# Making all adaLN vectors on TensorE and leaving GpSimd only its memsets, in a two-block transformer kernel

## The chip, the cores and the metric

The kernel runs on one core of one Trainium2 chip. The metric is the time of one execution on the device in microseconds (us), as the median of several runs. The core has five engines that matter here: TensorE (PE in the profile, its weight loads PEld), VectorE (DVE), ScalarE (ACT), GpSimd (POOL) and SyncE (SP), which issues all DMAs of this kernel. Each engine works through its own queue in order, and engines wait for each other by semaphores.

## The reference

Two transformer blocks of two layers each are applied to 256 tokens of 1024 features, in float32.

In a layer of the first block a conditioning vector `c` gives the adaLN vector `mod = silu(c) @ ada_w[l] + ada_b[l]`, 6144 numbers, which are split into six parts of 1024: a shift, a scale and a gate for the attention half, and the same for the MLP half. The attention half computes

```
h = rms_norm(x, norm1_g) * (1 + sc1) + sh1
da_q, da_k, da_v, dn_q, dn_k, dn_v, dn_z, dn_b, dn_a, gates = split(h @ w_in)
y_a = diff_attention(da_q, da_k, da_v, ...)
y_b = gated_deltanet(dn_q, dn_k, dn_v, dn_z, dn_b, dn_a, ...)
x = x + gt1 * ((g_a * (y_a @ w_branch_a) + g_b * (y_b @ w_branch_b)) @ w_out)
```

and the MLP half `x = x + gt2 * (relu(h @ w_mlp1)**2 @ w_mlp2)` with an `h` made of `sc2` and `sh2`. The delta rule works on chunks of 64 tokens: the inverse of a triangular matrix for each chunk, and then a scan over the four chunks, in both directions.

A layer of the second block has three kinds of attention over one projection, an output projection, and a mixture of 16 experts in which each expert picks 32 tokens; its weights are 12 MB an expert. The output is normed at the end.

## The kernel before

**Order of issue.** Nothing is issued as it is written. A class `Plan` records all operations of a stretch of the program, and a list schedule (`Plan.schedule`) then gives each engine, among the operations whose operands are there, the one with the longest way to the end by fixed costs and latencies. The first block is one such stretch. Every tile has a kind (`a8` 2048 columns, `s4` 1024, `w2` 512, `w1` 256, `t` 64, and the PSUM banks `acc` and `pg`), and the schedule also hands out the slots. In the first block there are five `a8` slots for loads of weights, eight `s4` slots for split weights, three `acc` banks for dense products and five `pg` banks for all else, and fourteen `w1` slots (8 and `W1X` = 6). Slots of `a8`, `s4` and `acc` are given out in program order.

**Weights.** A `Stream` holds the loads in the order of their use, 1 MB each. A weight that goes into a dense product is split in two fp32r halves: `act(hi, r)` on ScalarE and `tt(lo, r, hi, subtract)`, on VectorE or, by the table `LO`, on GpSimd:

```
LO = dict(dn=(V, G), gate=(V, V, G))
LO["in"] = (G, G, V)
```

`dense` then does three fp32r matmuls of 128x128 by 256 columns for each chunk of 128 rows.

**adaLN.** 48 units of 256 columns by 1024 rows. The first eight (the parts that the first norm needs) are loaded into `w2` tiles and done on TensorE: eight matmuls with `c32`, which is silu(c) repeated in 32 columns, fill four groups of 32 rows of a bank, and a product with `quad` adds up the groups. The other forty are items of the `Stream`: twelve of layer 0 between the loads of the attention stage, four of layer 0 and all 24 of layer 1 between the loads of layer 0's MLP. By `ADA` they go in turn to VectorE (a multiplication and seven multiply-adds of 128x256) and to GpSimd (one product of 128x2048 and three sums); four units' results are summed over the partitions by TensorE.

**A layer of the first block.** `Norm.finish` makes `h`; `dnp` makes the delta rule's q, k, v with a convolution (`conv`, VectorE); then `deltanet`'s steps are woven with `fill`, which holds the products for the differential attention, that attention itself (`diffattn`), the gates and `w_branch_a`. After that come `w_branch_b`, `w_out` with the residual add (`resid`), and the MLP in four quarters (`up`, `down`). In `deltanet`, GpSimd has the masks' products (`row`, `kkm`, `pd`, `cm`), `kb`, `kd`, the decay of the state and sums of the output; in `diffattn` the low halves of q and k; in the second block the low halves of the attention's outputs, `halves` (the normed tokens, split, for the gather) and small copies.

**The second block** has no `acc` banks; its `a8` slots take loads of expert weights that run ahead, and the tiles `xn`, `xh`, `xl` of `halves`.

In the profile nearly all instructions have line 596, where the schedule issues them; they are told apart by the names of tiles. There `block` is a tile of kinds `a8` and `s4`, `quarter` one of `w2`, `w` one of `w1`, `t` a small one, `ps` a PSUM bank, `x` the residual, `cT` silu(c), `mod` the adaLN vectors.

Of the kernel before, what the change touches and what calls it, by code (L numbers as in the profile page):

```python
# [10 lines left out]
F32R = mybir.dt.float32r  # L11
# [18 lines left out]
W1X, NT = 6, 10  # L30


# ---------------------------------------------------------------- host layout
def _units(w, n=2):
    """[K, N] -> [N/(128 n), 128 (k in chunk), n, K/128, 128]: lhsT units of n column chunks."""
    k, c = w.shape
    a = w.reshape(k // 128, 128, c // (128 * n), n, 128).transpose(2, 1, 3, 0, 4)
    return np.ascontiguousarray(a).reshape(c // (128 * n), 128, -1)


def _rows(w, kc):
    """[K, N] -> [K/(128 kc), 128, kc, N]: rhs units of kc row chunks."""
# [5 lines left out]
def _cols(v):  # L48
    """[n*128] -> [128, n]"""
    return np.ascontiguousarray(v.reshape(-1, 128).T)  # L50
# [13 lines left out]
def _shape_consts():  # L64
    """constants of the program, packed by the time that they are needed: c0 always, c1 and c2 per block"""
# [71 lines left out]
def _bias(rpb):  # L137
    """[4, 15, 31] -> [4, 128 (q in tile), 2 * 256]: bias of q over k, NEG outside q's window"""
# [10 lines left out]
def _layout(i):  # L149
# [25 lines left out]
    a["ada"] = st(lambda l: _rows_n(i["ada_w"][l], 256))  # L175
# [55 lines left out]
def _rows_n(w, n):  # L231
    """[1024, N] -> [N/n, 128, 8, n]"""
    k, c = w.shape
    a = w.reshape(8, 128, c // n, n).transpose(2, 1, 0, 3)
    return np.ascontiguousarray(a).reshape(c // n, 128, 8 * n)
# [35 lines left out]

class Tile:
# [7 lines left out]
class Plan:  # L280
    """Operations are recorded in program order and issued in the order of a list schedule: each engine takes,
    among the operations whose operands are there, the one with the longest way to the end. Costs and latencies
    are the guide's, in ns; they depend on shapes alone. A tile's slot is given out ahead of program order only if
    program order could still go on from there. Products that fill half of the array or less are not issued in long
    rows while others are ready: the array's clock falls when it is used little."""
# [17 lines left out]
    # -------------------------------------------------------- recording  # L303
# [22 lines left out]
    def box(r):  # L326
        """(what, partitions from, to, columns from, to)"""
# [37 lines left out]
    def add(self, eng, name, fn, args, kw):  # L365
# [4 lines left out]
        if eng == "P" and self.cols(ins[0]) < 128 and name == "matmul":  # L370
            p = self.ops[-1]
            rng = outs[0].ap.ap[0][1], outs[0].ap.offset // outs[0].ap.ap[0][0]
            if p.group and p.outs[0].t is outs[0].t and rng not in p.group:
                p.group.append(rng)
                self.access(p, n - 1, ins, outs)
                p.calls.append((fn, args, kw))
# [10 lines left out]
        o.eng, o.calls, o.dma, o.deps, o.succ, o.start, o.tiles = eng, [(fn, args, kw)], None, set(), [], None, []  # L387
# [38 lines left out]
    # -------------------------------------------------------- scheduling  # L426
# [3 lines left out]
    def keys(self, n0):  # L430
        """time to the end by a list schedule that runs backwards, in which every engine is single"""
# [33 lines left out]
    def schedule(self, slots):  # L465
        """slots: per kind of tile, the time at which each slot gets free"""
# [24 lines left out]
        def fit(e, t, dur):  # L491
            """the first time from t on at which engine e is idle for dur"""
# [8 lines left out]
        def can(i, t):  # L501
            """the earliest time from t on at which operation i's tiles have slots"""
# [76 lines left out]
    def flush(self, place, slots, issue):  # L579
        """schedules what has been recorded, into what waits and has gaps; place(kind, slot): the slot's memory"""  # L580
# [4 lines left out]
        for e in "PVAG":  # L585
            self.eng_at[e] = max(f for s, f in self.busy[e])
            self.busy[e] = []
        self.waiting.sort(key=lambda z: (self.ops[z[0]].start, z[0]))
        for i, place in self.waiting:
# [5 lines left out]
            for fn, args, kw in o.calls:  # L595
                self.tc.keep_in_program_order(fn(*map(real, args), **{k: real(v) for k, v in kw.items()}))  # L596
# [1545 lines left out]
```

## Time and profile before

| | |
|---|---|
| median of 3 runs | 2407.26 us (2403.64 to 2407.43) |
| profiled execution | span 2408.3 us, 38449 instructions |
| TensorE, weight loads | 82%, 60% of the span busy |
| VectorE | 48% |
| ScalarE | 33% |
| GpSimd | 19%, 278 instructions |
| mean granted TensorE clock | 0.862 of full speed |
| read from HBM | 617 MB |

The profiled execution is one execution of its own; its time is its span. Busy shares are means over stages that differ much, so they are read by stage below. A matmul's end is modelled, so a busy TensorE isn't TensorE at its peak.

### The profile page before, as it was taken

What the parts mean: (1) busy time and instruction counts of PE and PEld (TensorE: products, weight loads), DVE (VectorE), ACT (ScalarE), POOL (GpSimd) and SP (SyncE); (2) the same over time, 40 slices, a digit from 0 to 9 for tenths busy, and PEclk for the clock granted to TensorE, in tenths of its full rate; (3) what the DMA queues carried; (4) which work ended last, traced back from release to release, by engine and by line L of the source; (5) the groups of instructions that cost most, each with busy time, mean ns of one, the idle gap of its engine ahead of it and who ended that gap; (6) DMA issues with size and microseconds to landing.
All of it is one profiled execution on the core that took longest, in us unless ns stands there. A gap on an engine that the chain in (4) does not pass through costs nothing. (4 is left out here: it accounts for less than half of the span.)

```text
span 2408.3 us, 38449 instructions
## 1 busy us (share of the span) xinstructions
PE 1984.8 (82%) x16200; PEld 1437.7 (60%) x16200; DVE 1159.4 (48%) x1908; ACT 786.9 (33%) x1508; POOL 465.6 (19%) x278
## 2 busy tenths in 40 slices
PE   8688987778989999999999887666769988666665
PEld 5677777777987777999986542222237644222222
DVE  5998478999789623775557410000006731000001
ACT  4363343433457323654456210000015521000001
POOL 1555354455133312000020210000002111000000
PEclk7897898788999768999999888887779988877777
DMA  8354224566633310645544699999995579999997
GB/s 315 124 188 128 105 106 158 210 229 254 237 121 132 116 36 18 247 158 178 203 153 167 274 420 420 421 421 420 421 420 212 209 281 420 420 421 420 420 421 313
DMA packets 108253, 622.36 MB, mean 258 GB/s; under 512 B 27184, under 2 KB 28464, under 8 KB 34992
## 3 DMA queue, kind: packets, MB, share of 16 engines
q1 hardware_dynamic: 108080, 619.90, 65.4%
q8 instruction: 127, 2.08, 0.3%
q14 instruction: 46, 0.38, 0.0%
HBM read 617.24 MB, written 2.62 MB: 257 GB/s over the span
## 5 line engine op out<-in xcount | busy, mean ns | idle before, releaser
L596 PE MATMUL ps<-quarter,block 128*128 128x256 f32 (+1 forms) x5760 | 868.4, 304 | 72.5 <-DVE quarter L596 23.6
L596 PEld LDWEIGHTS ps<-quarter,block 128*128 128x128 f32 x5760 | 786.2, 205 | 114.9 <-issue 28.2
L596 PE MATMUL ps<-block,block 128*32 128x256 f32 (+4 forms) x5204 | 546.5, 431 | 137.9 <-DMA block<-in_w_up_dram 95.1
L596 PEld LDWEIGHTS ps<-block,block 128*32 128x32 f32 (+2 forms) x5204 | 274.4, 136 | 354.7 <-DMA block<-in_w_up_dram 159.3
L596 DVE TENSOR_TENSOR block<-block,block 128x1024 fp32r<-128x1024 f32 (+2 forms) x262 | 364.7, 1398 | 130.6 <-PE ps L596 73.1
L596 ACT ACTIVATE block<-block 128x1024 fp32r<-128x1024 f32 (+2 forms) x312 | 319.1, 1028 | 321.9 <-PE ps L596 292.8
L596 ACT ACTIVATE w<-ps 128x256 f32<-128x256 f32 (+1 forms) x138 | 52.3, 382 | 819.0 <-PE ps L596 818.9
L596 DVE TENSOR_TENSOR w<-w,ps 128x256 f32<-128x256 f32 x64 | 26.9, 421 | 544.3 <-ACT w L596 537.8
L596 POOL TENSOR_TENSOR block<-block,block 128x1024 fp32r<-128x1024 f32 x46 | 117.0, 2551 | 794.3 <-ACT block L596 387.8
L596 PE MATMUL ps<-block,w 128*32 128x256 f32 x2048 | 176.0, 500 | 25.8 <-ACT w L596 13.3
L596 PE MATMUL ps<-quarter,quarter 64*64 64x64 f32 (+6 forms) x1312 | 166.8, 304 | 6.9 <-DVE quarter L596 6.9
L596 PEld LDWEIGHTS ps<-block,w 128*32 128x32 f32 x2048 | 76.9, 142 | 116.2 <-issue 49.8
L596 PEld LDWEIGHTS ps<-quarter,quarter 64*64 64x64 f32 (+3 forms) x1312 | 113.2, 177 | 53.2 <-issue 20.0
L596 ACT ACTIVATE quarter<-quarter 128x512 f32<-128x512 f32 (+2 forms) x188 | 116.2, 628 | 85.0 <-DVE quarter L596 82.5
L596 ACT ACTIVATE quarter<-ps 128x512 f32<-128x512 f32 (+1 forms) x136 | 79.5, 592 | 151.2 <-PE ps L596 133.8
L596 DVE SCALAR_TENSOR_TENSOR w<-block,cT,w 128x256 f32<-128x256 f32 x140 | 126.5, 903 | 2.2
L596 DVE TENSOR_SCALAR w<-c,slot 128x256 f32<-128x256 f32 x32 | 12.5, 411 | 234.9 <-PE ps L596 234.8
L596 PE MATMUL ps<-w,w 32*128 32x256 f32 x512 | 106.7, 418 | 15.4 <-ACT w L596 15.1
L596 POOL TENSOR_TENSOR block<-block,cT 128x2048 f32<-128x2048 f32 x20 | 76.5, 3825 | 136.8 <-DVE w L596 41.0
L596 PEld LDWEIGHTS ps<-w,w 32*128 32x128 f32 x512 | 55.5, 185 | 69.2 <-issue 35.4
L596 DVE TENSOR_TENSOR quarter<-quarter,ps 128x512 f32<-128x512 f32 (+1 forms) x80 | 49.0, 629 | 84.7 <-PE ps L596 80.0
L596 POOL TENSOR_TENSOR block<-block 128x1024 f32<-128x1024 f32 (+1 forms) x40 | 85.2, 2131 | 2.4
(169 smaller groups left out, 1604.8 us busy)
## 6 DMA issues: line engine op xcount, KB each, us to landing
block<-in_w_gate_dram SPq DMA_DIRECT2D x144, 1024.0 KB, 19.8
block<-in_w_up_dram SPq DMA_DIRECT2D x128, 1024.0 KB, 19.8
block<-in_w_down_dram SPq DMA_DIRECT2D x128, 1024.0 KB, 19.8
block<-in_w_m_dram SPq DMA_DIRECT2D x64, 1024.0 KB, 4.8
block<-in_ada_dram SPq DMA_DIRECT2D x40, 1024.0 KB, 6.1
block<-in_w_dn_dram SPq DMA_DIRECT2D x16, 1024.0 KB, 4.8
block<-in_w_o_dram SPq DMA_DIRECT2D x16, 1024.0 KB, 7.0
block<-in_w_in_dram SPq DMA_DIRECT2D x12, 1024.0 KB, 12.1
```

The lines of the kernel that those rows point to most:

```text
L596: self.tc.keep_in_program_order(fn(*map(real, args), **{k: real(v) for k, v in kw.items()}))
```

## The change

All of adaLN goes to TensorE. The weights are laid out anew: a unit is now 256 rows by 1024 columns, so that four units make one of the six parts of 1024 columns. Each unit's eight matmuls add to one PSUM bank, which is held from the first of four units to the last; then one copy and two products with a four-column `quad` bring the rows into place, and one addition adds the bias. In the first block's `Stream` each layer now carries its own units 8 to 23, and layer 0's MLP the first eight of layer 1; in the MLP one comes after every second load and not after every load. All elementwise work of GpSimd goes to VectorE, memsets stay. `halves` does the scaling and the subtraction in one instruction, without the tile `xn`. `W1X` goes from 6 to 3. Besides, comments are gone, and each operation is issued by a function compiled at the line of its caller (`call_at`), so that the profile after names lines.

```diff
-W1X, NT = 6, 10
+W1X, NT = 3, 10
...
+def _ada(w):
+    a = w.reshape(4, 2, 128, 6, 1024).transpose(3, 0, 2, 1, 4)
+    return np.ascontiguousarray(a).reshape(24, 128, 2048)
...
-        LO = dict(dn=(V, G), gate=(V, V, G))
-        LO["in"] = (G, G, V)
...
-                        e = LO.get(key, (V,))
-                        tt(lo, r[:, h * n:h * n + n], f(hi), OP.subtract, e[self.ns % len(e)])
+                        tt(lo, r[:, h * n:h * n + n], f(hi), OP.subtract)
...
-        c32, quad = w1("c32"), tiny("quad", 1)
+        c32, quad = w1("c32"), one4[:, 128:132]
...
-            V.memset(quad[32 * j:32 * j + 1], 1.0)
+            V.memset(quad[32 * j:32 * j + 1, j:j + 1], 1.0)
...
+            def ada(l, u):
+                b, i = u // 4, u % 4
+
+                def go(r):
+                    if i == 0:
+                        held[l, b] = pgen()
+                    ps = held[l, b]
+                    for k in range(2):
+                        for j in range(4):
+                            w = (r[2 * k + j // 2][:, j % 2 * 256:j % 2 * 256 + 256] if isinstance(r, list) else
+                                 r[:, k * 1024 + j * 256:k * 1024 + j * 256 + 256])
+                            mm(ps[32 * j:32 * j + 32, 0:256], c32[:, 32 * (2 * i + k):32 * (2 * i + k) + 32], w,
+                               i + k == 0, i + k == 4)
+                    if i == 3:
+                        ps, row = held.pop((l, b)), w1("adar")
                         act(row, ps[:, 0:256])
                         ps = pgen()
                         for n in range(2):
+                            mm(ps[:, 4 * n:4 * n + 4], row[:, n * 128:(n + 1) * 128], quad)
+                        o = V1["ada_b"][0] + 8 * b
...
-            ADA = ((V, G), (G, V))
...
+                d = mix(d, [ada(l, u) for u in range(8, 20)], 2)
+                r = [(l, u) for u in range(20, 24)] + [(l + 1, u) for u in (4, 5, 6, 7, 0, 1, 2, 3) if l + 1 < DEPTH]
+                items += d + mix(e + m, [ada(a, b) for a, b in r], 2)
...
-                    tt(kkm[d], kk, bc(C[stct[d]], 8), OP.mult, G)
+                    tt(kkm[d], kk, bc(C[stct[d]], 8), OP.mult)
...
-                    xn, xh, xl = a8("xn"), a8("xh", F32R), a8("xl", F32R)
+                    xh, xl = a8("xh", F32R), a8("xl", F32R)
...
-                        G.tensor_scalar(xn[:, o], xt[:, t], r[:, t:t + 1], None, op0=OP.mult)
-                        tt(xl[:, o], xn[:, o], f(xh[:, o]), OP.subtract, G)
+                        stt(xl[:, o], xt[:, t], r[:, t:t + 1], f(xh[:, o]), OP.mult, OP.subtract)
```

The line of `kkm` stands for some twenty like it, in which only the engine is dropped.

## Rows read from the trace of the kernel before

**Rows 1.** Stages: length, busy us (count) of PE, PEld, DVE, ACT, POOL, clock, DMA share, GB/s.

```profile
45.00:220.00 175.00, 136.88 (x931) 121.67 (x930) 161.22 (x244) 84.09 (x142) 85.78 (x44) 0.86 0.44 154
220.00:428.00 208.00, 177.67 (x1337) 148.09 (x1337) 149.24 (x207) 78.48 (x155) 86.61 (x57) 0.85 0.36 129
428.00:678.00 250.00, 213.29 (x1613) 203.27 (x1612) 221.97 (x261) 98.93 (x142) 104.18 (x44) 0.90 0.60 227
678.00:826.00 148.00, 131.92 (x913) 116.99 (x913) 137.89 (x235) 86.81 (x145) 56.55 (x35) 0.91 0.35 121
826.00:1025.00 199.00, 197.60 (x1348) 160.64 (x1348) 92.27 (x159) 80.75 (x163) 25.72 (x27) 0.82 0.28 98
1025.00:1215.00 190.00, 187.34 (x1530) 185.76 (x1529) 116.09 (x151) 92.08 (x118) 5.76 (x2) 0.99 0.53 186
...
1356.00:1801.00 445.00, 322.57 (x3427) 139.70 (x3428) 24.63 (x60) 37.44 (x90) 10.28 (x4) 0.81 1.00 412
...
sum 2408.30, PE 1984.79 PEld 1437.73 DVE 1159.35 ACT 786.92 POOL 465.61; mean PE 180.44 PEld 130.70 DVE 105.40 ACT 71.54 POOL 42.33
```

**Rows 2.** Timeline at the ends of layer 0's stages: start, duration, instruction.

```profile
217.87 0.38 SPq L596 DMA_DIRECT2D xd<-quarter  x1
...
427.57 0.88 DVE L596 SCALAR_TENSOR_TENSOR x<-ps,mod,x 128x256 f32<-128x256 f32 x2 [1.32 <-PE ps L596]
...
677.49 0.88 DVE L596 SCALAR_TENSOR_TENSOR x<-ps,mod,x 128x256 f32<-128x256 f32 x2 [1.07 <-PE ps L596]
```

**Rows 3.** TensorE's dense products in the two MLPs: 428 to 678, 1025 to 1215.

```profile
L596 PE MATMUL ps<-quarter,block 128*128 128x256 f32 x1488 | 199.4, 297 | 28.2 <-DVE x L596 12.0 <-DVE block L596 8.9 <-ACT quarter L596 6.4
...
L596 PE MATMUL ps<-quarter,block 128*128 128x256 f32 x1488 | 182.2, 285 | 2.7 <-ACT quarter L596 1.7 <-DVE quarter L596 0.9
```

**Rows 4.** VectorE's groups by form: 428 to 678, 1025 to 1215, whole run (count | busy, mean ns).

```profile
L596 DVE TENSOR_TENSOR block<-block,block 128x1024 fp32r<-128x1024 f32 x63 | 97.8, 1566 | 22.1 <-PE ps L596 10.6 <-ACT block L596 9.7 <-issue 0.9
L596 DVE SCALAR_TENSOR_TENSOR w<-block,cT,w 128x256 f32<-128x256 f32 x77 | 74.9, 972 | 1.4
...
L596 DVE TENSOR_TENSOR block<-block,block 128x1024 fp32r<-128x1024 f32 x60 | 73.4, 1225 | 64.5 <-PE ps L596 50.1 <-ACT block L596 13.0 <-issue 1.2
...
L596 DVE SCALAR_TENSOR_TENSOR w<-block,cT,w 128x256 f32<-128x256 f32 x140 | 126.5, 903 | 2.2
```

**Rows 5.** Timeline of GpSimd and VectorE around 476.

```profile
475.70 3.60 POOL L596 TENSOR_TENSOR block<-block,cT 128x2048 f32<-128x2048 f32 x1 [10.48 <-DVE quarter L596]
...
476.69 3.69 DVE L596 TENSOR_TENSOR block<-block,block 128x1024 fp32r<-128x1024 f32 x1 [0.93 <-issue]
```

**Rows 6.** GpSimd's groups by form, whole run (adaLN's are four, first and last shown).

```profile
L596 POOL TENSOR_TENSOR block<-block,block 128x1024 fp32r<-128x1024 f32 x46 | 117.0, 2551 | 794.3 <-ACT block L596 387.8 <-DMA block<-in_w_in_dram 371.9 <-DVE block L596 16.7
L596 POOL TENSOR_TENSOR block<-block,cT 128x2048 f32<-128x2048 f32 x20 | 76.5, 3825 | 136.8 <-DVE w L596 41.0 <-DMA block<-in_ada_dram 40.8 <-DVE quarter L596 37.1
...
L596 POOL TENSOR_TENSOR w<-block 128x256 f32<-128x256 f32 x20 | 25.4, 1272 | 6.5 <-DVE quarter L596 5.4
...
L596 POOL MEMSET quarter<- 128x512 f32 x16 | 8.4, 541 | 44.8 <-PE ps L596 38.9 <-DVE quarter L596 5.3 <-DMA lb<-quarter 0.5
```

**Rows 7.** Timeline of TensorE in the start-up: sets of eight ada products.

```profile
13.43 1.08 PE L596 MATMUL ps<-quarter,w 128*32 128x256 f32 x8
...
28.02 0.64 PE L596 MATMUL ps<-quarter,w 128*32 128x256 f32 x8
```

**Rows 8.** Timeline of TensorE: sets of eight and single dense products by turns.

```profile
1361.09 0.64 PE L596 MATMUL ps<-block,block 128*32 128x256 f32 x8
...
1361.66 0.39 PE L596 MATMUL ps<-w,block 128*128 128x256 f32 x1
...
1361.98 0.64 PE L596 MATMUL ps<-block,block 128*32 128x256 f32 x8
```

**Rows 9.** Timeline of SP's queue before the first gather.

```profile
1337.88 1.99 SPq L596 DMA_DIRECT2D block<-in_w_up_dram  x4
...
1362.68 3.27 SPq L596 DMA_DIRECT2D block<-in_w_down_dram  x4
```

More of the change, by code (lines that the diff above doesn't have):

```diff
@@ L1 @@
 import math
+import sys
 from bisect import bisect
@@ L174, in _layout @@
     st = lambda fn: np.stack([fn(l) for l in range(DEPTH)])
-    a["ada"] = st(lambda l: _rows_n(i["ada_w"][l], 256))
+    a["ada"] = st(lambda l: _ada(i["ada_w"][l]))
     a["w_daqk"] = st(lambda l: _units(w[l][:, 0:1024]))
@@ L269, in real, with line, call_at @@
         return x
+HELPERS = {"act", "tt", "ts", "stt", "mm", "sigm", "<lambda>"}
+CALLS = {}
+def line():
+    f = sys._getframe(2)
+    while f.f_code.co_name in HELPERS:
+        f = f.f_back
+    return f.f_lineno
+def call_at(n):
+    if n not in CALLS:
+        space = {}
+        exec(compile("\n" * (n - 1) + "def call(fn, a, k): return fn(*a, **k)", __file__, "exec"), space)
+        CALLS[n] = space["call"]
+    return CALLS[n]
 class Tile:
@@ L386, in add @@
             o.small = name == "matmul" and min(k, n_) <= 64
-        o.eng, o.calls, o.dma, o.deps, o.succ, o.start, o.tiles = eng, [(fn, args, kw)], None, set(), [], None, []
+        o.eng, o.calls, o.dma, o.deps, o.succ, o.start, o.tiles = eng, [(fn, args, kw, line())], None, set(), [], None, []
         if eng == "S":
@@ L585, in flush @@
         for e in "PVAG":
-            self.eng_at[e] = max(f for s, f in self.busy[e])
+            self.eng_at[e] = max([f for s, f in self.busy[e]], default=self.eng_at[e])
             self.busy[e] = []
@@ L594, in flush @@
             real = lambda x: x.real() if isinstance(x, Ref) else x
-            for fn, args, kw in o.calls:
-                self.tc.keep_in_program_order(fn(*map(real, args), **{k: real(v) for k, v in kw.items()}))
+            for fn, args, kw, n in o.calls:
+                self.tc.keep_in_program_order(
+                    call_at(n)(fn, tuple(map(real, args)), {k: real(v) for k, v in kw.items()}))
         self.waiting = []
@@ L911, in _build @@
             vview = lambda l: {k: v1[l][:, o:o + n] for k, (o, n) in V1.items()}
-            part = []
-            def ada(l, u, e):
+            held = {}
+            def ada(l, u):
+                b, i = u // 4, u % 4
                 def go(r):
-                    if e is PE:
-                        ps, row = pgen(), w1("adar")
-                        for k in range(8):
-                            j = k % 4
-                            mm(ps[32 * j:32 * j + 32, 0:256], c32[:, 32 * k:32 * k + 32], r[k // 2][:, k % 2 * 256:k % 2 * 256 + 256],
-                               k < 4, k >= 4)
+                    if i == 0:
[9 more added lines that the diff above has]
+                        ps, row = held.pop((l, b)), w1("adar")
                         act(row, ps[:, 0:256])
@@ L986, in _build @@
                     m += [("m" + q, A["w_m" + q][l, i + u], "split") for u in range(4)]
-                if l == 0:
-                    d = mix(d, [ada(0, u, ADA[0][u % len(ADA[0])]) for u in range(8, 20)], 2)
-                    r = [(0, u) for u in range(20, 24)] + [(1, u) for u in range(24)]
-                    r = [ada(a, b, ADA[1][j % len(ADA[1])]) for j, (a, b) in enumerate(r)]
-                    em = mix(e + m, r, 1)
-                else:
-                    em = e + m
-                items += d + em
+                d = mix(d, [ada(l, u) for u in range(8, 20)], 2)
+                r = [(l, u) for u in range(20, 24)] + [(l + 1, u) for u in (4, 5, 6, 7, 0, 1, 2, 3) if l + 1 < DEPTH]
+                items += d + mix(e + m, [ada(a, b) for a, b in r], 2)
             st = Stream(items)
@@ L1014, in add @@
                     if 0 < self.n < 3:
-                        tt(self.sq, self.sq, q, OP.add, G)
+                        tt(self.sq, self.sq, q, OP.add)
                     else:
@@ L1436, in deltanet @@
                         else:
-                            tt(ot[t][hv[a]], ot[t][hv[a]], tmp[hv[a]], OP.add, G)
+                            tt(ot[t][hv[a]], ot[t][hv[a]], tmp[hv[a]], OP.add)
                     yield 1
@@ L1560, in _build @@
                     SY.dma_start(x, A["ada"][0, u][:, 512 * i:512 * i + 512])
-                ada(0, u, PE)[2](r)
+                ada(0, u)[2](r)
             for k in range(8):
```

65 lines of the change are left out of this document (17 added, 48 removed).

## The prediction, made before the change was run

> **What bounds the kernel now.** Read first the busy time of each engine by stage [rows 1]. The stages are cut at marks of the trace [rows 2]: the last residual add after `w_out` of layer 0 at 428, the last one of its MLP at 678, and inside the attention stage the write of the inverted blocks (`xd`) at 218. The same marks of layer 1 end the windows at 826, 1025 and 1215. So the first block's layer 0 takes 45 to 678 and layer 1, with the same products, 678 to 1215: 633 us against 537. The second block follows, with expert weights that keep the DMA engines at a share of 1.00 in 1356 to 1801.
>
> Set the stages of the two layers beside each other. Both MLPs do the same 1488 dense products [rows 3]. Layer 1's needs 190 us, with TensorE busy for 187 of them at clock 0.99 and waiting 2.7 us; layer 0's needs 250 us, with TensorE waiting and slower (0.90), and VectorE busy for 222 us of it [rows 1]. So layer 1's MLP is bound by TensorE and layer 0's by VectorE. The attention stages say the same, less loudly: 175 us against 148 up to the inverse, 208 against 199 behind it; VectorE is busy 161 of 175 and 138 of 148 in the first halves, TensorE 198 of 199 (at clock 0.82) in layer 1's second half.
>
> Then look at what VectorE's time is made of. One form, the low half of a weight (128x1024), takes 1225 ns in layer 1's MLP, where GpSimd is all but idle, and 1566 ns in layer 0's [rows 4]. The timeline shows the cause: at 475.70 GpSimd starts a product of 3.60 us; a VectorE subtraction that begins at 476.69 takes 3.69 us [rows 5] in place of 1.2. Where both engines read SBUF, VectorE stands still while GpSimd's instruction runs. GpSimd's 465.6 us are therefore not free help: they are paid a second time on VectorE.
>
> **The change, part by part.** (a) *adaLN off VectorE and GpSimd.* Twenty streamed units leave VectorE: 140 multiply-adds of 903 ns, 126.5 us in the whole run, of which 74.9 lie in layer 0's MLP [rows 4]. Twenty leave GpSimd: four groups of instructions, 187 us in sum [rows 6].
>
> (b) *The rest of GpSimd's work goes to VectorE.* 465.6 less 187 is at most 279 us there. The commonest moved form takes 2551 ns on GpSimd [rows 6] and 1225 ns on an undisturbed VectorE [rows 4], a ratio of 0.48, so VectorE gets some 134 us. In number of microseconds (a) and (b) cancel (-126 and +134). What VectorE gains is that nothing stops it any more: 63 such halves in layer 0's MLP alone are 341 ns too long each, 21 us. GpSimd keeps sixteen memsets, 8.4 us [rows 6]; they could stop VectorE for that long at most, and not at all at least; I take nothing, since they are 2% of what it did. The Trainium skill (SBUF — State Buffer, "Who interferes with whom") says that a VectorE instruction with two SBUF inputs contends with a GpSimd one that reads SBUF and not with one that only writes it; no row here shows the memset case, and by that page the 8.4 us would be zero.
>
> (c) *adaLN on TensorE.* The kernel does it already for its first eight units, so the price is in the trace: eight matmuls take 0.64 us at full clock and 1.08 us at half [rows 7]. Forty units give 26 to 43 us. Interleaved with other shapes a set of eight and one dense matmul repeat every 0.89 us (1361.09 to 1361.98) [rows 8], 0.57 and 0.32 of it. A dense matmul costs 0.12 (182.2 us for 1488, [rows 3]), so a set in such company costs up to 0.77. I take 0.8 a unit, 32 us in all, of which only that counts which falls where TensorE sets the pace. If a unit is cut into two sets, with 0.2 us (0.32 less 0.12) lost at each, 16 us come on top over forty units. The small products that move four rows into columns, and the partition sums that they replace, are about equal in number (two of four columns a block against four sums and two transposes), so I cost them at nothing; two single products of 0.39 us a block [rows 8] would be 8 us over ten blocks, if nothing left in exchange. The Trainium skill (TensorEngine Tiling, "Key Properties") says that changing the tiling mode drains TensorE, which speaks against cutting 128x32 products into a dense stream. The trace agrees in kind: the dense matmul between two sets takes 0.32 us and not 0.12.
>
> (d) *Order and space.* Layer 1's twelve units of the attention stage and four of the MLP move from layer 0's MLP into layer 1; 12 MB more pass there, at a DMA share of 0.28 to 0.35 [rows 1], which hides them; with that cover gone a megabyte is 2.5 us (at 412 GB/s, [rows 1]). A unit's block (five slots) is given back after under 1 us of TensorE instead of some 9 us of GpSimd (187 us over 20, [rows 6]) or 6.3 of VectorE (seven of 903 ns), so weight loads behind it on SP's queue start earlier. A new wait stands on TensorE: a set waits for its load, and the dense products queued behind it wait too, and with them ScalarE and VectorE, which empty their banks. GpSimd waited 40.8 us for such loads [rows 6], on a queue that held nothing urgent. Of that at most the part in stages where weights are late would pass to TensorE; I take nothing, since blocks come back sooner, and 10 us (a quarter) as the bound. Against the gain, one of the five general PSUM banks is held over four units, nearly all through both attention stages, and small scratch tiles fall from fourteen to eleven (four that held partial sums are gone, so I cost that at nothing). The trace has no stage with four banks. Bounds: nothing, and the 36 us by which layer 0's attention stage exceeds layer 1's with everything that disturbs it now, for both stages together; layer 1, with few ada tiles about, waits little, so I take 5.
>
> (e) *Second block.* Splits of the input weights leave GpSimd: 1.3 us less (2.55 against 1.23) for a half that TensorE waits for at the start of each layer; 2 us in sum, 0 to 4. `halves` no longer needs the block `xn`. Before the gather the loads stop for want of blocks: the last four are issued at 1337.88, the next at 1362.68 [rows 9]. One more block lets one more megabyte come early, 2.5 us (1.05 MB at 412 GB/s), in each of two layers if it goes to a load: 0 to 5, I take 4. The two multiply-subtracts of 1.2 us that VectorE takes over lie beside ScalarE and the top-k; at worst they delay the gather by 2.4 us a layer, 5 us.
>
> **The sum,** by stage: layer 0 up to the inverse, from 175 towards layer 1's 148 with the split contention gone too: -26 (-15 to -33). Layer 0 behind it, 208 towards 199 plus five units: -6 (-14 to +4). Its MLP: 250 to layer 1's 190 plus twelve units of 0.8: -50 (-38 to -57). Layer 1 up to the inverse: VectorE's 138 of 148 lose the stalls and gain GpSimd's 56.6 x 0.48 = 27; TensorE's 132 gain seven units, 6 us: 148 to 142, -6 (-14 to +6). Layer 1 behind it, TensorE bound: five units less a shorter chain (1.2 for 2.5 us a step): +3 (-5 to +6). Its MLP: +3. Second block: -6 (-11 to +5). Bank: +5 (0 to 36). Start-up has its eight ada units on TensorE now as later, and doesn't move. In all -83. The profiled execution has a span of 2408.3 us and nothing shown around it; the median of the timed runs is 2407.3, 1.0 less. 2407.3 - 83 = **2324 us**.
>
> **Rivals.** (A) *TensorE pays more than I think*: drains at each switch of shape, clock drops and the missing bank. The 16 us of (c) and the bank's 36 in place of 5 make +47: **2371**. For it: three of the six stages show a clock of 0.82 to 0.86 [rows 1]. Against: layer 0's MLP gains 50 by VectorE alone, whatever these cost. (B) *VectorE stays the bound*, because its long durations have another cause than GpSimd. Of GpSimd's 255 us in the four attention stages [rows 1] about half of the 187 are adaLN's; the other 161 cost VectorE 77 at 0.48, and 100 if its instructions stay as long as in layer 0 (1566 for 1225). The first halves, bound by VectorE, would show half of that, 50 us: **2374**. Against: the timeline of [rows 5]. (C) *Slower*: the held PSUM bank decides. In both attention stages scores take two banks, one bank stays with the outputs and the delta rule takes two or more; with four left, attention and delta rule run behind each other. It turns the gain into a loss from 44 us a stage on (88 of 383 and 347 us); at 60 us a stage the time is **2439**. Against: TensorE is busy 198 of 199 us in layer 1's second half, so a bank has to cost a great deal. (D) *More than I think*: with TensorE never starved, clock 0.85 goes to 0.95 in the attention stages (730 us); if TensorE sets the pace in half of them, 365 x (1 - 0.85/0.95) is 38 us more: **2286**. (E) *No change*: GpSimd and VectorE hidden anyway; [rows 3] exclude it nearly.
>
> **How the numbers follow.** Forecast (2295 to 2350) 0.62; A 0.14; B 0.08; D 0.10; C 0.04; E 0.02. A measurement of this kernel tells 0.2% (5 us) from no change. Range: 2280 to 2375, which leaves out C, E, and the far ends of D and A. Faster 0.94, same 0.02, slower 0.04.
>
> **What would show it.** In the profile after: low halves of 1.22 us in every stage; VectorE near 125 us busy in layer 0's MLP; that stage at about 200 us with TensorE's clock near 0.98; POOL under 10 us; ada sets of 0.6 to 0.9 us. Wrong if layer 0's MLP stays above 220 (another bound), if a layer's attention stage grows beyond 350 us (bank or drains), or if TensorE's waits on ada tiles appear.

## The result, and the profile after

The changed kernel takes 2325.85 us (median of 4 runs, 2313.76 to 2338.03) against 2405.45 us before (4 runs, 2402.72 to 2407.43): a ratio of 0.9665, 95% interval 0.9618 to 0.9713. The forecast was 2324. The times fall in two groups with nothing between them: of eight executions (four more of the same kernel follow below) three lie at 2313.8 to 2319.2 us and five at 2334.1 to 2338.0. So the median of the first four, two of either group, lies where no execution does; the median of all eight is 2335.1. The profiled one is of the upper group (span 2336.2 us, 72 less than before); what the traces say of the 20 us between the groups comes further down.

Busy time of each engine by stage, cut at the same marks as [rows 1] (length, then busy us and count of PE, PEld, DVE, ACT, POOL, then TensorE's clock, DMA share, GB/s):

```profile
45.00:191.00 146.00, 134.74 (x1016) 113.37 (x1014) 114.86 (x241) 82.58 (x136) 0.00 (x0) 0.93 0.52 183
191.00:391.50 200.50, 196.43 (x1482) 155.80 (x1482) 105.82 (x192) 82.33 (x164) 2.63 (x5) 0.84 0.36 124
391.50:596.00 204.50, 203.68 (x1709) 192.83 (x1708) 124.04 (x174) 97.14 (x139) 0.00 (x0) 1.00 0.58 211
596.00:747.00 151.00, 137.48 (x1007) 115.55 (x1006) 121.15 (x258) 86.73 (x148) 0.00 (x0) 0.92 0.47 158
747.00:945.00 198.00, 193.64 (x1495) 153.88 (x1494) 105.64 (x194) 81.72 (x163) 0.00 (x0) 0.86 0.36 126
945.00:1134.00 189.00, 187.29 (x1544) 185.93 (x1543) 116.21 (x152) 91.31 (x118) 0.00 (x0) 1.00 0.56 200
```

Against [rows 1], layer 0's MLP went from 250 to 204.5 us. VectorE, busy 222 of the 250, is now busy 124 of 204.5; TensorE is busy nearly throughout, at clock 1.00. Layer 0's MLP is now bound by TensorE, as layer 1's was before. In the first halves of the attention TensorE has some room left (busy 135 of 146 and 137 of 151), and VectorE is busy for 115 and 121 us of them.

The totals of the page and its group of low halves; below them, from the timeline, one adaLN unit among dense products in layer 0:

```profile
PE 1994.8 (85%) x16756; PEld 1418.2 (61%) x16756; DVE 979.8 (42%) x1912; ACT 785.9 (34%) x1502; POOL 8.1 (0%) x20
...
L789 DVE TENSOR_TENSOR block<-block,block 128x1024 fp32r<-128x1024 f32 (+1 forms) x296 | 358.2, 1215 | 242.3 <-ACT block L788 122.9
```

```profile
168.34 0.64 PE L946 MATMUL ps<-block,w 128*32 128x256 f32 x8
168.91 0.39 PE L830 MATMUL ps<-quarter,block 128*128 128x256 f32 x1
169.23 0.64 PE L946 MATMUL ps<-block,w 128*32 128x256 f32 x8
169.80 0.39 PE L830 MATMUL ps<-quarter,block 128*128 128x256 f32 x1
```

All 296 low halves in the run now take 1215 ns on average (two shapes), where [rows 4] had 1566 in layer 0's MLP. The two sets of eight are *one* unit: line 946 leaves 640 records from 45 to 1134 us for forty units of eight products, two for each product, sixteen a unit. I had read a set of eight [rows 7] as a whole unit. By stage the units lie 7, 9 and 9 in layer 0 (up to the inverse, behind it, MLP) and 6, 9 and none in layer 1; the forecast had 7, 5, 12 and 7, 5, 4.

What TensorE waited for from 45 to 1134 us (total, times, longest):

```profile
PE ps L1268 <- ACT quarter L1270: 21.2, 4, 8.8
PE ps L827 <- ACT quarter L1068: 4.0, 2, 2.0
...
PE ps L946 <- DMA block<-in_ada_dram: 1.0, 1, 1.0
```

The wait for adaLN tiles that the prediction watched for is 1.0 us. Its other sign, an attention stage beyond 350 us, was nearly met: layer 1's takes 349. The largest wait is a new one, 21.2 us in four pieces, at the transposes of k and v (line 1268).

### The profile page after: what moved, and what is told of

Same layout as the page of the kernel before. It is cut to its first block, busy times and chain, and to the rows that moved or that the text cites. A ratio compares the mean times of both kernels' runs of the same rounds, so it can differ in the third digit from the quotient of the medians.

```text
span 2336.2 us, 39136 instructions
## 1 busy us (share of the span) xinstructions
PE 1994.8 (85%) x16756; PEld 1418.2 (61%) x16756; DVE 979.8 (42%) x1912; ACT 785.9 (34%) x1502; POOL 8.1 (0%) x20
## 4 chain that ended last, share of the span: by engine, by line
PE 59%; DMA 31%; DVE 5%; ACT 4%; issue 1%; SPq 0%; DVEq 0%; ACTq 0%
PE ps L827 11%; PE ps L828 11%; PE ps L830 11%; DMA block<-in_w_up_dram 10%; DMA block<-in_w_down_dram 10%; DMA block<-in_w_gate_dram 9%; PE ps L2070 2%; PE ps L1313 2%; PE ps L2086 2%; PE ps L946 2%; PE ps L2093 1%; DMA quarter<-in_ada_dram 1%; PE ps L2045 1%; PE ps L1485 1%; PE ps L1409 1%; DMA block<-in_w_in_dram 1%
## 5 line engine op out<-in xcount | busy, mean ns | idle before, releaser
L827 PE MATMUL ps<-quarter,block 128*128 128x256 f32 x1856 | 463.2, 296 | 6.3 <-ACT quarter L1068 4.0
L828 PE MATMUL ps<-quarter,block 128*128 128x256 f32 x1856 | 461.0, 296 | 5.8 <-DVE quarter L1629 2.1
L2070 PE MATMUL ps<-block,block 128*32 128x256 f32 x4096 | 343.1, 453 | 140.7 <-DMA block<-in_w_up_dram 96.2
L789 DVE TENSOR_TENSOR block<-block,block 128x1024 fp32r<-128x1024 f32 (+1 forms) x296 | 358.2, 1215 | 242.3 <-ACT block L788 122.9
L788 ACT ACTIVATE block<-block 128x1024 fp32r<-128x1024 f32 (+1 forms) x296 | 310.1, 1050 | 331.9 <-PE ps L828 221.8
L830 PE MATMUL ps<-quarter,block 128*128 128x256 f32 x1856 | 408.1, 294 | 1.2 <-DVE block L789 1.1
L827 PEld LDWEIGHTS ps<-quarter,block 128*128 128x128 f32 x1856 | 327.9, 196 | 29.0 <-issue 11.1
L828 PEld LDWEIGHTS ps<-quarter,block 128*128 128x128 f32 x1856 | 327.5, 196 | 22.9 <-issue 9.1
L830 PEld LDWEIGHTS ps<-quarter,block 128*128 128x128 f32 x1856 | 318.6, 194 | 17.1 <-issue 6.5
L2070 PEld LDWEIGHTS ps<-block,block 128*32 128x32 f32 x4096 | 116.9, 123 | 328.2 <-DMA block<-in_w_up_dram 159.5
L2074 DVE TENSOR_TENSOR w<-w,ps 128x256 f32<-128x256 f32 x32 | 13.5, 421 | 572.5 <-ACT w L2073 572.5
L2073 ACT ACTIVATE w<-ps 128x256 f32<-128x256 f32 x32 | 12.3, 383 | 512.4 <-PE ps L2070 497.6
L2089 ACT ACTIVATE w<-ps 128x256 f32<-128x256 f32 x32 | 12.3, 383 | 203.3 <-PE ps L2086 203.3
L2078 PE MATMUL ps<-c,w 128*128 128x128 f32 x64 | 19.7, 398 | 68.3 <-DVE w L2075 68.3
L827 PE MATMUL ps<-block,block 128*128 128x256 f32 x160 | 50.4, 338 | 8.3 <-ACT block L788 8.3
L1313 PE MATMUL ps<-quarter,quarter 64*64 64x64 f32 x640 | 56.0, 318 | 0.3 <-DVE quarter L1303 0.3
```

The costliest lines, as they stand in the source:

```text
L788: act(hi, r[:, h * n:h * n + n])
L789: tt(lo, r[:, h * n:h * n + n], f(hi), OP.subtract)
L827: mm(o, hi[:, j, k], xhi(k), k == 0, False)
L828: mm(o, hi[:, j, k], xlo(k), False, False)
L830: mm(o, lo[:, j, k], xhi(k), False, k == kc - 1)
L1313: mm(ps[r, q], lh[r, q], rh[r, q])
```

## The experiments

Stage lengths in us, from the windows of each trace cut at that kernel's own marks; for the stages behind the inverse also TensorE's clock. Each column is one profiled execution. The column "forecast" gives the change that the prediction gave the stage. "Router" is the stretch from the first block's end to the second block's first router norm; the -6 forecast beside it was for the whole second block.

| stage | before | after | forecast | adaLN only | elementwise only | no held bank | two banks |
|---|---|---|---|---|---|---|---|
| layer 0, to the inverse | 173 | 146 | -26 | 140.5 | 170 | 136.5 | 136.5 |
| layer 0, behind it | 210 (0.85) | 200.5 (0.84) | -6 | 203.5 (0.91) | 219 (0.79) | 195 (0.85) | 193.5 (0.90) |
| layer 0, MLP | 250 | 204.5 | -50 | 202.5 | 256 | 205.5 | 205 |
| layer 1, to the inverse | 146.5 | 151 | -6 | 146.5 | 139 | 140.5 | 144.5 |
| layer 1, behind it | 201 (0.82) | 198 (0.86) | +3 | 192 (0.89) | 179 (0.87) | 175.5 (0.98) | 204 (0.85) |
| layer 1, MLP | 190 | 189 | +3 | 189 | 190 | 189.5 | 191 |
| router | 127.5 | 137 | -6 | 129 | 135 | 136.5 | 136 |
| median of all | 2405 to 2410 | 2326, 2335 | 2324 | 2320 | 2412 | 2291 | 2323 |

**The changed kernel once more** (no edit).

> The changed kernel itself, once more. Its four runs fell at 2313.8, 2314.9, 2336.8 and 2338.0 us. If these are two levels of one program, new runs fall near 2314 or near 2337 again and the granted clock goes with them (0.89 against 0.874); if it is scatter, they lie between.

2335.11 us (2319.18 to 2336.72), ratio 0.9671 (0.9633 to 0.9710). Three of four runs lie in the upper group at clocks 0.875 to 0.877, one at 2319.18 at 0.886. Two levels, then, and the clock goes with them. The execution traced here is of the upper group again (span 2334.4 us), and each of its stages is within 1.5 us of the first trace's, layer 1 behind the inverse among them:

```profile
746.00:943.50 197.50, 193.16 (x1492) 153.40 (x1492) 105.19 (x192) 81.68 (x162) 0.00 (x0) 0.86 0.36 126
```

**AdaLN alone, elementwise work alone.** The first puts all elementwise work back on GpSimd; the second keeps that on VectorE and takes back adaLN's old code, order and weights' layout.

```diff
+        LO = dict(dn=(V, G), gate=(V, V, G))
+        LO["in"] = (G, G, V)
...
-                    tt(kkm[d], kk, bc(C[stct[d]], 8), OP.mult)
+                    tt(kkm[d], kk, bc(C[stct[d]], 8), OP.mult, G)
```

> Only adaLN on TensorE; GpSimd keeps the masks' products, the low halves of LO, halves, the copies. Theory (VectorE was the bound in layer 0 because adaLN sat on it and on GpSimd, which stops it): layer 0's MLP takes 205 us as in the changed kernel, since no other work of GpSimd lies there, low halves in it take 1.22 us; layer 0's attention stage becomes like layer 1's of before (148 and 200 us) plus nothing; the second block's first layer is at its old 128 us from the last residual add to the router's rms. So about 2320 us, no slower than the changed kernel: adaLN alone carries the gain. Rival (the rest of GpSimd's work stops VectorE as much): low halves in the attention stages stay at 1.4 us and more, the two attention stages together 15 to 30 us longer than in the changed kernel, 2340 to 2355 us.

```diff
+            ADA = ((V, G), (G, V))
...
-                d = mix(d, [ada(l, u) for u in range(8, 20)], 2)
+                if l == 0:
+                    d = mix(d, [ada(0, u, ADA[0][u % len(ADA[0])]) for u in range(8, 20)], 2)
```

> Only the elementwise work moved to VectorE; adaLN stays on VectorE and GpSimd, in the old places. Theory: layer 0's MLP stays at 245 to 255 us with low halves at 1.5 us and more, since the adaLN products are the only work of GpSimd there; layer 0's attention stage, where VectorE was busy 161 of 173 us, gets longer or stays (370 to 395 us); the second block's first layer is 9 us longer as in the changed kernel. In all 2400 to 2425 us, no gain. Rival (elementwise work on GpSimd is what costs): 2360 us or less.

AdaLN alone: 2319.9 us, ratio 0.9640 (0.9616 to 0.9663), the whole gain. Elementwise work alone: 2411.85 us (ten runs, 2400.58 to 2415.85), 1.0016 (1.0001 to 1.0032), none. Layer 0's MLP of the two kernels, and layer 0's first half of the first:

```profile
45.00:185.50 140.50, 128.70 (x963) 109.44 (x961) 125.70 (x219) 83.40 (x133) 51.67 (x32) 0.94 0.50 173
...
389.00:591.50 202.50, 201.66 (x1689) 191.86 (x1688) 122.18 (x171) 97.64 (x140) 5.65 (x4) 1.00 0.58 208
```

```profile
434.00:690.00 256.00, 216.66 (x1628) 206.07 (x1628) 227.04 (x267) 98.91 (x143) 100.03 (x48) 0.90 0.60 226
```

With adaLN off both engines the MLP drops to 202.5 us; with adaLN left there it stays at 256, VectorE busy for 227. The low halves in it take 1228 ns on average without adaLN on GpSimd and 1546 with it. In the first half GpSimd's 51.7 us are still there, and still stop VectorE (126 us for 219 instructions, against 115 for 241 in the changed kernel); this does not lengthen the stage, since VectorE has room. In the trace of elementwise work alone layer 1's attention, where no adaLN work lies, is shorter (318 us against 347.5); layer 0's attention and MLP (6 us each) and the router stretch (7.5) give most of it back. That trace is of the fastest of the ten runs, so the 29.5 us rest on one execution. VectorE's time over the whole run shows what the elementwise move does to it: 962 us busy with that work on GpSimd (adaLN alone), 980 with it on VectorE (the changed kernel). VectorE took over GpSimd's other work and needed only 18 us more.

**The second block's input weights' low halves on GpSimd again** (`LO["in"] = (G, G, V)` alone).

> The changed kernel, but with two in three low halves of the second block's input weights on GpSimd as before. Theory: in the changed kernel TensorE waits at the start of that block for low halves that stand on VectorE behind a series of 3.25 us, and the clock falls to half after it; with them on GpSimd the 137 us from the last residual add of the first block to the router's rms become 128 to 130, and the time falls by 7 to 9 us at the same clock of the first block. Rival (it is the order of the schedule, not the engine): the stretch stays at 134 to 140.

2328.5 us, 0.9693 (0.9645 to 0.9742); the router stretch is 134.5 us. My theory falls: these halves alone give 2.5 us there. Between the two routers the kernel loses 9.5 (603.5 us against 594), so that the edit does not pay as a whole; the cause of that stays open. But this kernel issues the same instructions in the first block, in the same order on TensorE, VectorE and ScalarE, as the changed kernel, and so shows something else. Layer 1 behind the inverse, two windows of 12 us first (PE's busy time, clock, DMA share, GB/s), then the whole stage; the changed kernel, then this one:

```profile
771.00:783.00 12.00, 12.00 (x100) 0.50 0.26 89
783.00:795.00 12.00, 12.00 (x104) 0.50 0.00 1
```

```profile
768.00:780.00 12.00, 12.00 (x157) 1.00 0.25 89
780.00:792.00 12.00, 12.00 (x108) 1.00 0.26 85
...
744.00:925.00 181.00, 176.00 (x1482) 140.98 (x1481) 104.86 (x190) 81.76 (x162) 0.00 (x0) 0.96 0.40 137
```

The changed kernel's TensorE ran at half clock from 761 to 809 us although it was busy nearly throughout (its second trace has the same 48 us); with the same work in the same order the other execution stayed at full clock there, and its stage took 181 us in place of 198. The 17 us are close to the step of 20 between the two groups of the result. This kernel's own runs show that step too: three at 2326.8 to 2329.6 us, the traced one among them, and one at 2349.3. That the step is this stretch is likely and not shown: no execution of the changed kernel's lower group was traced.

**No bank held.** Each unit is summed in a bank that is given back at once; VectorE adds up in SBUF.

```diff
-                    if i == 0:
-                        held[l, b] = pgen()
-                    ps = held[l, b]
+                    ps = pgen()
...
+                    if i == 0:
+                        held[l, b] = w1("adar")
+                        V.tensor_copy(held[l, b], ps[:, 0:256])
+                    else:
+                        tt(held[l, b], held[l, b], ps[:, 0:256], OP.add)
```

> The changed kernel, but every adaLN unit is summed in a PSUM bank of its own, given back at once, and VectorE adds the four results up in SBUF (40 copies and additions of some 0.4 us, 17 us on an engine that isn't the bound). If the held bank costs what the prediction took (5 us) or more (up to 36), the attention stages, 346 and 349 us in the changed kernel, get shorter by that. If it costs nothing, they stay within 3 us or get a little longer by the 40 extra additions.

2290.9 us (2286.61 to 2302.80), 0.9533 (0.9499 to 0.9568): 35 to 44 us less than the changed kernel's two medians, some 25 less than its lower group. The attention stages are 331.5 and 316 us, and the wait at the transposes is gone. Layer 1 behind the inverse has the largest part, 175.5 for 198; but the same stage took 181 us with the bank held and the order unchanged, in the execution above that kept its clock. What that wait was, in the changed kernel's timeline, and TensorE's busy time and clock around it (windows):

```profile
121.92 0.60 PE L1268 MATMUL ps<-c,quarter 128*128 128x128 f32 x4
...
123.69 5.77 ACT L870 ACTIVATE quarter<-quarter 32x512 f32<-32x512 f32 x9
129.48 0.69 ACT L1586 ACTIVATE quarter<-ps,v 128x512 f32<-128x512 f32 x1
130.06 0.59 ACT L1270 ACTIVATE quarter<-ps 128x512 f32<-128x512 f32 x1
...
130.71 1.12 PE L1268 MATMUL ps<-c,quarter 128*128 128x128 f32 x4 [8.19 <-ACT quarter L1270]
```

```profile
114.00:126.00 12.00, 8.52 (x74) 1.00 0.55 180
126.00:139.50 13.50, 6.72 (x22) 0.50 0.19 74
```

The second four transposes wait 8.19 us for the copy (line 1270) that empties the first four's bank, and ScalarE has nine rotary copies of 0.6 us in front of it. The windows below it show the clock at half for 13.5 us from the middle of the wait on. So the bank looked guilty; the doubling that follows tests that.

**Two banks held.**

```diff
-                        held[l, b] = pgen()
+                        held[l, b] = [pgen(), pgen()]
...
-                        act(row, ps[:, 0:256])
+                        act(row, ps[0][:, 0:256])
+                        tt(row, row, ps[1][:, 0:256], OP.add)
```

> The changed kernel with two PSUM banks held in place of one: the two row chunks of a unit add to a bank each, and one addition more joins them. If a held bank is what the attention stages pay for (346 and 349 us with one, 331 and 316 without), two cost as much again or more: 360 to 400 us each, 2360 to 2430 us in all. If the gain without the bank came from another order of the schedule, the stages stay within 10 us of one bank's.

2323.02 us (2311.78 to 2324.16), 0.9626 (0.9594 to 0.9657); attention stages 330 and 348.5 us. Not slower than with one bank. A price for each held bank is excluded. Nor does the wait at the transposes come with a held bank: here, with two, it is gone, layer 0's first half takes 136.5 us as with none, and TensorE waits 19.1 us, in two pieces, for VectorE at another place (line 1238). What is left is that the bank changes the order that the schedule makes; no run changes the order and nothing else, so this is argued.

**Layer 1's sixteen units in layer 0's MLP**, where they were before.

```diff
-                d = mix(d, [ada(l, u) for u in range(8, 20)], 2)
+                r = []
+                if l == 0:
+                    d = mix(d, [ada(l, u) for u in range(8, 20)], 2)
+                    r = [(0, u) for u in range(20, 24)] + [(1, u) for u in (4, 5, 6, 7, 0, 1, 2, 3, *range(8, 24))]
```

> The changed kernel with layer 1's last sixteen adaLN units in layer 0's MLP, as they were before the change, and not in layer 1. A unit is sixteen matmul records in the trace after, 1.29 us of TensorE. Theory 1 (a unit costs its TensorE time wherever TensorE sets the pace): layer 0's MLP 205 + 15 x 1.25 = 224 us, layer 1's attention stage 349 - 19 = 330 us, nothing in sum. Theory 2 (units among the small products of an attention stage cost more than their own time; elementwise work alone on VectorE gave 139 and 179 us there without adaLN, 31 us less): layer 1's attention stage 318 to 325, 8 to 14 us faster in sum.

2318.93 us, 0.9639 (0.9623 to 0.9655). Layer 0's MLP is 223 us, +18.5 for the 13 more units that lie there (352 of its ada records against 144), 1.4 each, of which 1.28 is their own time; layer 1's attention is 330.5. Both as Theory 1 has it. The MLP's window:

```profile
367.00:590.00 223.00, 222.22 (x1922) 198.09 (x1920) 119.92 (x173) 95.90 (x140) 0.00 (x0) 1.00 0.68 253
```

This splits the MLP's gain. The kernel before had 22 units in this stage as well (77 multiply-adds of VectorE [rows 4] are eleven, GpSimd had as many), and 22 are here. With the same units and loads in the stage, the other engine alone brings it from 250 us to 223, with TensorE busy nearly throughout; so the loads were not the bound. The other 18.5 us come from moving thirteen units out, and layer 1's attention pays for that (349 us against 330.5).

Layer 0's attention, in which the edit moves nothing, changed as well: behind the inverse it went from 200.5 us at clock 0.84 to 179 at 0.96, with two units more in it (176 records for 144). How much of that is the order, and how much a clock that one order can get either way, was not separated.

**The same order with GpSimd's elementwise work kept.**

> A candidate: adaLN on TensorE with GpSimd's elementwise work left on GpSimd, which took 2319.9 us, and layer 1's sixteen units in layer 0's MLP. If units among an attention stage's products cost more than in the MLP, 8 to 14 us less than 2319.9; if not, the same within 5 us.

2360.9 us, 0.9814 (0.9797 to 0.9831): a miss, 41 us slower than adaLN alone. Its stages behind the inverse take 215.5 us at clock 0.84 and 208 at 0.81.

**Useless work on GpSimd.**

```diff
+                    if nm in ("m1", "m2"):
+                        scr = w2("scr")
+                        if 2 * self.done < len(self.items):
+                            for _ in range(2):
+                                G.tensor_tensor(scr, c0[:, 0:512], c0[:, 128:640], op=OP.mult)
+                        else:
+                            for _ in range(5):
+                                G.memset(scr, 0.0)
```

> The changed kernel with useless work on GpSimd in the MLPs: in layer 0's two products of 128x512 for each weight (64, some 80 us), in layer 1's five memsets of 128x512 (160, some 87 us). Theory (VectorE stands still while GpSimd reads SBUF, and not while it only writes): low halves of layer 0's MLP 1.45 us and more in place of 1.22, those of layer 1's MLP 1.22 as now; both stages stay at 205 and 189 us, since VectorE has 80 us to spare. Rival (the long low halves of before had another cause, waits or addresses): 1.22 in both. Third (memsets stop it as well): longer in both.

2364.44 us (two runs, 2358.66 and 2370.22). The split fell by place in the list, so 27 weights got products (54, 78.3 us) and 37 memsets (185), and the schedule issued both far ahead of the MLPs. The stages named were not tested, but two others were: all products fell into layer 0's attention up to the inverse, two in three memsets behind it. Windows of these two stages, then lines of the timeline, then the convolution's multiply-adds (one form) in the first stage, here and in the changed kernel:

```profile
45.00:241.50 196.50, 143.96 (x995) 120.83 (x994) 168.20 (x240) 81.48 (x133) 92.88 (x82) 0.80 0.39 135
241.50:423.00 181.50, 176.50 (x1485) 141.72 (x1484) 105.04 (x190) 81.65 (x162) 64.95 (x124) 0.96 0.39 137
```

```profile
122.83 6.61 POOL L789 TENSOR_TENSOR quarter<-c 128x512 f32<-128x512 f32 x4
126.03 2.28 DVE L797 TENSOR_TENSOR block<-block,block 128x1024 fp32r<-128x1024 f32 x1
...
418.61 5.77 POOL L792 MEMSET quarter<- 128x512 f32 x10
421.21 1.23 DVE L797 TENSOR_TENSOR block<-block,block 128x1024 fp32r<-128x1024 f32 x1 [0.53 <-ACT quarter L1024]
```

```profile
L1183 DVE SCALAR_TENSOR_TENSOR quarter<-quarter,v,quarter 128x255 f32<-128x255 f32 x24 | 26.7, 1149 | 0.0
```

```profile
L1175 DVE SCALAR_TENSOR_TENSOR quarter<-quarter,v,quarter 128x255 f32<-128x255 f32 x24 | 10.6, 478 | 0.0
```

With the products VectorE is busy 168.2 us for 240 instructions, where the changed kernel has 114.9 for 241, and the stage is 50.5 us longer. With 65 us of memsets it is busy 105.0 us for 190 instructions, as without them (105.8 for 192). One low half takes 2.28 us beside products (the longest of 32 in the stage; most ran after the products) and 1.23 beside memsets. The largest part of the 53 us is the convolution's: its multiply-adds take 1149 ns on average in place of 478. So GpSimd's products, which read SBUF, lengthen VectorE's instructions, and its memsets, which only write, do not. The useless work also holds a 512-column slot each time; that could lengthen waits, but not VectorE's busy time.

**Three candidates without a held bank:** the second block's elementwise work on GpSimd; all of it on GpSimd; layer 1's units in layer 0's MLP.

> The kernel without the held bank (2290.9 us), with the second block's elementwise work back on GpSimd (two in three low halves of its input weights, the low halves of its attention outputs, halves, the small copies). Theory (the move to VectorE is what made that block's first stretch 136.5 us in place of 127.5; adaLN alone had 129.0): 127 to 129 us again, the time 8 us less, some 2283 us. Rival (order of the schedule): 134 or more, no gain; the low halves alone gave 1.7 us.

> Without the held bank, and all elementwise work back on GpSimd. With adaLN alone on TensorE and the bank held, that work on GpSimd cost nothing (2319.9 against 2326 to 2335). Theory 1 (TensorE sets the pace in the attention stages, so GpSimd's stops of VectorE are hidden): 2280 to 2290 us. Theory 2 (with a bank more VectorE's chain decides there): the four attention half stages, 136, 195, 141 and 175 us without the held bank, grow by 10 us and more in sum, 2295 to 2310.

> Without the held bank, layer 1's sixteen units in layer 0's MLP. A unit in the MLP costs its TensorE time (223 for 205 us with 15 more: 1.2 us each). If the held bank was what the units cost in layer 1's attention stage, nothing is left to gain: 2290 us within 8. If they cost something besides, that stage falls from 316 to 300 or less and the time with it.

The first: 2288.24 us, 0.9484 (0.9453 to 0.9515), the fastest kernel by its ratio. Its router stretch, beside the changed kernel's:

```profile
1092.00:1219.50 127.50, 123.77 (x725) 96.18 (x723) 90.04 (x204) 78.77 (x191) 21.81 (x14) 1.00 0.45 173
```

```profile
1133.50:1270.50 137.00, 126.50 (x729) 100.37 (x727) 97.01 (x221) 80.86 (x192) 0.00 (x0) 0.95 0.46 172
```

The 9 us are back. The expected 8 us of the whole are not shown (2288.24 against 2290.9, within the spread of both); the profiled execution gives 4.5 of them back in the next stretch, up to the second router (595.5 us against 591).

The second: 2341.63 us, 0.9713 (0.9694 to 0.9733), a miss. Its first halves are short (129.5, the shortest of all, and 141), but behind the inverse it takes 224.5 us at clock 0.80 and 208 at 0.90. The third: 2295.39 us, 0.9530 (0.9508 to 0.9551), as expected where the units cost the same in either place; layer 1's attention is 308 us, between the two expectations.

## Why the prediction was right, and where its terms were off

**VectorE was the bound, and GpSimd stopped it: shown.** The prediction read that from the two MLPs [rows 3, 4] and one overlap [rows 5]. AdaLN alone gives the MLP's 47 us, elementwise work alone none, and the useless products lengthen VectorE's time by 53 us. Rival B falls. Two things qualify it. About 20 of the 47 us went into layer 1 with the units that moved there; 27 are the engine's. And adaLN burdened VectorE in two ways, by its own multiply-adds there (74.9 us in this stage [rows 4]) and by GpSimd's stops (some 21 us on the low halves); no run takes away one without the other. The memsets, for which no row stood, cost nothing. The Trainium skill (SBUF — State Buffer, "Who interferes with whom") says that a VectorE instruction with two SBUF inputs contends with a GpSimd instruction that reads SBUF and not with one that only writes it; the trace agrees: 2.28 us beside products, 1.23 beside memsets.

**The three terms of layer 0** were -26, -6 and -50, measured -27, -9.5 and -45.5. The second is inside its range although nine units lie there and not five; its own terms (208 towards 199, and five units of 0.8) make -5 and not -6. The MLP's miss of 4.5 us is in part the price of a unit: twelve at 0.8, 9.6 us, were forecast; nine lie there (144 records), at 1.25 of their own time (11.3 us) or 1.4 in all (12.8). The term that was mis-sized is (c), "eight matmuls take 0.64 us" taken for a unit; forty units keep TensorE busy for 51.5 us, not 26 to 43. The switch of shape costs as expected: a dense product between two sets takes 0.32 us (168.91 to 169.23), as in [rows 8].

**Step (b), that elementwise work on VectorE helps because nothing stops it:** true of VectorE's durations, not of the time. Of the 134 us that VectorE was to get, 18 are left net of the stops that are gone (980 us busy against 962). But in this kernel the half that carries it gave nothing (2319.9 us without it, 2326 and 2335 with it).

**Step (e) failed, and outside its range.** -6 (-11 to +5) was forecast, +9.5 measured. I had costed GpSimd's work there as slow help and not as work done beside VectorE. The whole of the second block is 10 us longer, and all of that lies in the router stretch. At that block's start eight multiply-subtracts, 3.25 us together, stand on VectorE ahead of the first low half, and TensorE waits 3.28 us for it:

```profile
1133.65 3.25 DVE L1833 SCALAR_TENSOR_TENSOR block<-x,v,block 128x256 fp32r<-128x256 f32 x8
...
1136.81 1.22 DVE L789 TENSOR_TENSOR block<-block,block 128x1024 fp32r<-128x1024 f32 x1
...
1138.08 0.38 PE L813 MATMUL ps<-block,block 128*128 128x256 f32 x1 [3.28 <-DVE block L789]
```

The 3.28 us are a third of the 9.5. With all of that block's elementwise work on GpSimd the stretch is 127.5 us again; which part of it besides the low halves does it was not separated.

**Layer 1:** -6, +3, +3 forecast, +4.5, -3, -1 measured; the first two are inside their ranges, the second by an execution that lost 17 us to the clock there. The third was four units, and none lies in that MLP. VectorE got free there as forecast (busy 121 us of 151), but about half of TensorE's 21.2 us of waits at the transposes came in its place.

**The bank's +5 (0 to 36)** has no single measurement. Rival C fell (346.5 and 349 us of attention, where 60 more a stage would be 443 and 407). The kernel without a held bank is some 25 us below the changed kernel's lower group and 35 to 44 below its medians; taking a second bank cost nothing. Both are shown; what links them is argued: the attention stages' length hangs on the order that the list schedule lands on, by its waits and its clock. With one bank held, another placing of the units gives layer 0's attention 322 us in place of 346.5, less than the 331.5 with none. Length times clock behind the inverse lies at 156 to 187 us in all these kernels (198 x 0.86 = 170, 175.5 x 0.98 = 172, 208 x 0.81 = 168), while the lengths run from 174 to 224.5: the clock has a large part in the differences, not the whole. Why the clock falls under one order and not under another, and sometimes under the same one, stays open. Rival A was right in that TensorE pays more for the units, and too high in sum; D's clock of 0.95 is what the kernel without the held bank gets in three of four attention stages.

So the mechanism was right in the stage that gave most, and the closeness of 2324 to 2325.85 is luck: the terms erred to both sides (the second block's start is 15 us worse than forecast, layer 1 up to the inverse 10.5, the MLP 4.5), and the median lies between two groups. The profiled execution gained 72 us where 83 were forecast, the lower group of runs some 90.

## What to carry to other kernels

Find the stage with the same work done twice, once with an engine in the way and once without, and forecast the slow one by the fast one: that gave 76 of the 83 us forecast here, and 72.5 were measured in these two stages. Split a change that does two things before crediting both: here adaLN earned the whole gain, and the elementwise move was free at best. Where a list schedule gives the order and the clock varies, stages that an edit does not touch move by 20 us, so test a suspected resource by doubling it too, not only by taking it away, and trace more than one execution before a stage's length is put down to the edit.

## What the runs showed of the hardware

With the same instructions in the same order, TensorE's granted clock fell to half for 48 us in two executions and stayed full in a third (198 and 197.5 against 181 us for the stage), while the engine was busy in all. GpSimd's memsets leave VectorE's two-input instructions alone (105.0 us with 65 us of memsets, 105.8 without), its products do not (168.2 against 114.9). The products lengthen a multiplication of one SBUF tile by a value for each partition too (128x256, twelve in the stage: 795 ns on average with the useless work, 349 without). One fp32 product of 128x32 by 256 columns leaves two records, and so does one of 128x128 by 4 columns (line 953, twenty products and forty records from 45 to 1134 us), so a count of records is not a count of products.
